# Layer 0's keys and values turned to rows by VectorE in 32x32 blocks instead of by TensorE

## The chip, the cores and the metric

The kernel runs on one core of a Trainium2 chip, in one launch. The metric is the time of the program on the device in microseconds (us); the core's engines (TensorE, VectorE, ScalarE, GpSimd, SyncE; PE, DVE, ACT, POOL and SP in the profile) run side by side, each through its own queue of instructions in order.

## What is computed

One step of a two-layer streaming encoder with 2,048 channels, for 512 new tokens of a prompt and 16 new tokens of each of 8 running streams (640 tokens in all). Layer 0 is stick-breaking attention, layer 1 gated linear attention. What matters here is the start of layer 0:

```python
h = rmsnorm(x, norm_g[i]) * (1 + scale[:, None]) + shift[:, None]
q, k, v, zg = jnp.split(h @ w_in, 4, axis=-1)          # each (tokens, 2048)
...
new_k.append(k)                                        # outputs: rows of tokens
new_v.append(v)
```

The keys `k` and the values `v` of all 640 tokens are outputs, token by token, as rows of 16 heads of 128 channels. The scale, shift and gate come from products of a conditioning vector with the matrix `w_ada`.

## The kernel before, in words

The projections of layer 0 are computed transposed: TensorE multiplies a block of the weight (as the stationary side) with the transposed activations, so that a result has channels on the 128 partitions and tokens along the free axis. `by_sevens` does this for 256 output channels at a time, with seven products in place of eight (a Strassen-like scheme over two halves of the tokens and two of the channels). One round of its loop is called a **job** here. A job has seven **products** of 24 matmuls (L592), each 320 tokens wide. Its result is `out`, two tiles of 128 channels by 640 tokens: `out[0]` is complete after the sixth product, `out[1]` after the seventh. There are 28 jobs in layer 0: for each of the eight pairs of heads the keys (K0 to K7) and the queries, from pair 2 on the values too (V2 to V7; those of pairs 0 and 1 are made elsewhere), and at the end six jobs of the gate. The order is K0 Q0 K1 Q1 K2 Q2 V2 K3 Q3 V3 and so on to V7.

A job's weights are four loads of 512 KB, issued by SP: three into tiles named `wb` (four buffers) and one into `wr`. Each waits until an earlier tile has been split into a high and a low part (ACT, L134, and DVE, L135), and a split waits until TensorE has freed a pair of split tiles. So the first `wb` of a round can go soon after the end of the job before, `wr` later, and the next `wb` only after the second product.

Beside the jobs two kinds of side work run, as lanes that a small planner (`Side`, with a clock of TensorE's work in the program) drops between half products. `rest_of_ada` multiplies `w_ada` with the conditioning vectors: 56 groups of eight short matmuls (L180 and L222), five half products apart, each of which uses two tiles `ar` of 512 KB. There are two `ar` buffers, so the loads for a group can start only when the group before is done. The lane has work up to job K7. The other lane is `as_rows`: after a key or value job it turns `out` to rows of tokens, in three steps one half product apart. A step has four (the last one two) transposes of 128x128 on TensorE into PSUM (L677); DVE copies the result to a tile `kr` (L858), and SP stores it (L74): `kr` to the output, and for values to the scratch tensor `vd` as well, which the attention reads later. A store moves rows of 256 channels, 1 KB at a time. The keys are also stored as they are, without a turn, to `kd` (`keep_in`).

The order of TensorE's instructions is the program's. Those of the other engines are put in order by a scheduler when the program is built. SP's queue is one queue: weight loads, `ar` loads and stores are issued in one order, and an instruction that waits holds up all behind it.

Of the kernel before, what the change touches and what calls it, by code (L numbers as in the profile page):

```python
# [8 lines left out]
F32 = mybir.dt.float32  # L9
# [6 lines left out]
P = 128  # L16
D = 2048
KT = D // P
NP = 512
# [22 lines left out]
def hybrid_step_kernel(ctx: ExitStack, tc: tile.TileContext, A: dict, O: list):  # L42
# [4 lines left out]
    dve = nc.vector  # L47
# [17 lines left out]
    def block(x):  # L65

        pe["now"] += 0.11
        return x
# [4 lines left out]
    def store(out, in_):  # L73
        nc.sync.dma_start(out=out, in_=in_)  # L74

    def move(out, in_):

        nc.gpsimd.dma_start(out=out, in_=in_)
# [20 lines left out]
    def bank(tag):  # L99
        return psum["pool"].tile([P, 512], F32, tag=tag, name=f"ps_{tag}", bufs=psum["bufs"][tag])  # L100
# [28 lines left out]
    v_d = [dp.tile([T, 256], F32, name=f"vd_{p}") for p in range(NPAIR)]  # L129
# [136 lines left out]
    def slot(n, shape=(P, T), dt=F32R, name="h"):  # L266
        return hp.tile(list(shape), dt, tag=f"t{n}", name=name)
# [6 lines left out]
    def step(wait=0.0, tp=0, z=0, tiled=False):  # L274
        return wait, tp, z, tiled

    class Side:
# [21 lines left out]
        def next(self, lane):  # L299
            what = next(lane[0], None)  # L300
            if what is None:
                self.lanes.remove(lane)
            else:
                lane[1] = (pe["now"] + what[0], {"tp": what[1], "z": what[2]}, what[3])
# [4 lines left out]
        def run(self, x):  # L309
            taken = {k: n for k, n in x[1][1].items() if n}  # L310
            self.next(x)
            for k, n in taken.items():
                f = sorted(self.free[k])
                self.free[k] = f[n:] + [pe["now"] + self.hold[k]] * n
# [29 lines left out]
    side = Side()  # L344

    def drive(*gens):
        for g in gens:
            for _ in g:
                side.tick()
# [311 lines left out]
    def keep_in(d):  # L661
        def f(out):
            for hh in range(2):
                store(d[:, hh, :], out[hh])
        return f

    def as_rows(out, leave):

        for g in range(3):
            yield step(3.0 if g == 0 else 0.5, tp=1)  # L670
            n = min(2, TOK - 2 * g)
            tp = bank("tp")
            for a in range(n):
                for hh in range(2):
                    c = 256 * a + P * hh
                    t0 = P * (2 * g + a)
                    turn_block(tp[:, c:c + P], block(out[hh][:, t0:t0 + P]), ident)  # L677
            leave(g, n, tp[:, :256 * n].rearrange("p (a n) -> p a n", n=256))
# [60 lines left out]
    kp_rows = kp_o.rearrange("l b t h d -> (l b t) (h d)")  # L739
    vp_rows = vp_o.rearrange("l b t h d -> (l b t) (h d)")  # L740
    ks_rows = ks_o.rearrange("l b t h d -> (l b t) (h d)")
    vs_rows = vs_o.rearrange("l b t h d -> (l b t) (h d)")
# [9 lines left out]
    with tc.tile_pool(name="st", bufs=1, reuse_waits="tile") as st:  # L752
# [21 lines left out]
        for a in range(TOK):  # L774
            ss4 = st.tile([P, 4], F32, tag="ss4", name="ss4", bufs=2)
            for q in range(4):
# [3 lines left out]
                tp = bank("mm")  # L780
# [8 lines left out]
            if a == 2:  # L789
                tp = bank("tp")  # L790
# [53 lines left out]
    def rest_of_ada():  # L844
        yield step(22.0)
        yield from ada_gate(ad, ad_ring, 0, "z", 2, cT)
        for k0 in range(0, 8, 2):
            yield from ada_mod(ad, ad_ring, 1, k0, 2, "z", 2)
        yield from ada_gate(ad, ad_ring, 1, "z", 2, cT, (0,))

    with tc.tile_pool(name="wq", bufs=1, reuse_waits="tile") as wq:
        def rows0(out, p, scratch, prompt, sample):

            cs = slice(256 * p, 256 * p + 256)

            def leave(g, n, tp):
                kr = slot(12 + g % 2, (P, 2, 256), F32, "kr")
                dve.tensor_copy(kr[:, :n, :], tp)  # L858
                if scratch is not None:
                    store(scratch[256 * g:256 * g + P * n, :].rearrange("(a p) n -> p a n", p=P), kr[:, :n, :])  # L860
                if g < 2:
                    store(prompt[256 * g:256 * g + 256, cs].rearrange("(a p) n -> p a n", p=P), kr)
                else:
                    store(sample[:, cs], kr[:, 0, :])

            return as_rows(out, leave)

        def keep_key(p):
            def f(out):
                keep_in(k_d[p])(out)  # L870
                side.add(rows0(out, p, None, kp_rows, ks_rows))
            return f

        def keep_value(p):
            return lambda out: side.add(rows0(out, p, v_d[p], vp_rows, vs_rows))

        jobs = []
        for p in range(NPAIR):
            jobs += [(D + 256 * p, keep_key(p)), (256 * p, keep_in(q_d[p]))]
            if p >= 2:  # L880
                jobs.append((2 * D + 256 * p, keep_value(p)))
        jobs += [(3 * D + 256 * p, keep_in(z_d[p])) for p in range(PLAIN, NPAIR)]
        side.every = 8.0
        side.add(rest_of_ada())
        ring3["pool"] = wq
        ring3["n"] = 0
        sevens = by_sevens(h1, w_in0, wq, jobs, given)
        for _ in range(2):
            next(sevens)
        for i in range(5):  # L890
            v01 = slot(8 + i, (P, 512), F32, "v01")
            (dve.tensor_copy if i % 2 else nc.scalar.copy)(v01, acc[i])
            for p in range(2):
                move(v_d[p][P * i:P * i + P, :], v01[:, 256 * p:256 * p + 256])
            move(vp_rows[P * i:P * i + P, 0:512] if i < 4 else vs_rows[:, 0:512], v01)
        ends.close()
        drive(sevens)
        side.finish()
        h1.again(0, wq)
        ring3["pool"] = None  # L900
# [326 lines left out]
    with tc.tile_pool(name="o0", bufs=1, reuse_waits="tile") as po, ExitStack() as only_d:  # L1227
# [3 lines left out]
        t = sp.tile([P, 1280], F32, tag="s2", name="c1")  # L1231
# [3 lines left out]
        t = sp.tile([P, 512], F32R, tag="s7", name="middles")  # L1235
# [184 lines left out]
        for nt in range(2):  # L1420
            x = low[nt][:32, :HALF]
# [28 lines left out]

        jobs = [(NK, keep_in(gk_d[0]))]
        jobs += [(2 * NK + 512 * h + 256 * n, keep_value(h, n)) for h in range(1, GH) for n in range(2)]
        jobs += [(2 * NK + D + 512 * h + 256 * n, keep_gate(h, n)) for h in range(GH) for n in range(2)]
        sevens = by_sevens(h2, w_in1, wq, jobs)
        next(sevens)
        n = 0
# [37 lines left out]
    with tc.tile_pool(name="gl", bufs=1, reuse_waits="tile") as gl:  # L1494
# [30 lines left out]
        t = mask_g[1].rearrange("p (b t) -> p b t", b=NB)  # L1525
# [61 lines left out]
        def leave(h, t0, on, g):  # L1587

            tp = bank("tp")
            for s in range(4):  # L1590
                turn_block(tp[:, P * s:P * s + P], block(on[:, P * s:P * s + P]), ident)
            dve.tensor_tensor(g, tp.rearrange("p (s t) -> p s t", s=4), g, op=ALU.mult)
            move(og_d[h][:, :, t0:t0 + P], g)
# [332 lines left out]
    with tc.tile_pool(name="o1", bufs=1, reuse_waits="tile") as po:  # L1926
# [3 lines left out]
        for kt in range(10, 16):  # L1930
            r = po.tile([P, T], F32, tag="rows", name="og_in", bufs=6)
            load(r, og_d[kt // 4][:, kt % 4, :])
            n = 20 + 2 * kt % 12
# [88 lines left out]
```

## Time and profile before

| | us |
|---|---|
| median of three runs (lowest, highest) | 2547.45 (2543.54, 2550.54) |
| the profiled execution: its time, and its span | 2556.43, 2554.7 |
| TensorE busy | 2442.0 (96%) |
| VectorE busy | 1582.3 (62%) |
| ScalarE busy | 995.3 (39%) |
| DMA queue of SP: share of the 16 DMA engines over the span | 54.4% |

The busy shares say that TensorE is what the kernel waits for nearly everywhere. Busy time of TensorE counts overlapping matmuls once; in the groups by line, a matmul's own duration overlaps with its neighbours', so what one costs is read from the distance of starts in the timeline. In a row of the timeline the columns are start, duration, engine, line, operation, tiles (written <- read), shape and count. The stage that the change touches, from K0's first transpose to V7's, lies between 187 and 794 us.

### The profile page before, as it was taken

Reading aid. Unit: us, or ns where it says so; the run is one execution under the profiler, and the core shown is the slowest. Engines: PE = TensorE matmul, PEld = TensorE weight load, DVE = VectorE, ACT = ScalarE, POOL = GpSimd, SP = SyncE. Lnnn points to the kernel's source line nnn. Section 1 sums busy time; section 2 is a strip of 40 time slices with the busy share of each in tenths; the row PEclk is TensorE's granted clock in tenths of the full one; section 3 lists DMA queues with packets and bytes.
Section 4 is the critical chain, followed back from the end, with each engine's and each line's share of the span. In section 5 each row is a group of like instructions: output and inputs, shape, how many; then the busy total and the mean of one; then the engine's idle time right before and its main releaser. Section 6 shows DMA issues by size and latency. Waiting matters only on the chain.

```text
span 2554.7 us, 43975 instructions
## 1 busy us (share of the span) xinstructions
PE 2442.0 (96%) x17561; PEld 2159.4 (85%) x17561; DVE 1582.3 (62%) x2565; ACT 995.3 (39%) x1730; POOL 164.1 (6%) x390
## 2 busy tenths in 40 slices
PE   6899999999999989999999989999999999979998
PEld 4589999998999989788887767999999988857776
DVE  5575555555666656666775677666766465555456
ACT  4332222222223334555442354333333464455223
POOL 0010000000000000000000000000000233243100
PEclk8899999999999999999999989999999999989999
DMA  9966666766654357778764753344444677785634
GB/s 341 321 211 210 223 212 201 239 215 196 220 186 122 118 188 236 248 245 253 255 211 123 232 184 114 105 121 139 118 115 117 209 230 244 228 283 191 210 117 147
DMA packets 469439, 503.13 MB, mean 197 GB/s; under 512 B 42730, under 2 KB 366450, under 8 KB 469106
## 3 DMA queue, kind: packets, MB, share of 16 engines
q1 hardware_dynamic: 446274, 436.60, 54.4%
q0 software_dynamic: 16048, 51.92, 6.1%
q10 hardware_dynamic: 6912, 11.80, 1.2%
q8 instruction: 138, 2.26, 0.4%
q14 instruction: 67, 0.55, 0.1%
HBM read 411.10 MB, written 89.13 MB: 196 GB/s over the span
## 4 chain that ended last, share of the span: by engine, by line
PE 77%; DMA 7%; DVE 5%; ACT 3%; issue 2%; POOL 0%; SPq 0%; ACTq 0%; POOLq 0%; DVEq 0%
PE ps_mm L592 39%; PE ps_mm L696 10%; PE ps_mm L650 7%; PE ps_mm L367 3%; PE ps_tp L1079 2%; PE ps_tp L1544 2%; DMA gv<-kr 1%; PE ps_mm L516 1%; PE ps_tp L1131 1%; PE ps_tp L1039 1%; PE ps_z L1015 1%; PE ps_z L180 1%; PE ps_mm L1993 1%; PE ps_z L1093 1%; PE ps_z L222 1%
## 5 line engine op out<-in xcount | busy, mean ns | idle before, releaser
L592 PE MATMUL ps_mm<-sums,wh 128*128 128x320 f32 x2752 | 616.5, 313 | 3.8 <-ACT wh L134 3.8
L592 PEld LDWEIGHTS ps_mm<-sums,wh 128*128 128x128 f32 x2752 | 460.8, 189 | 12.9 <-issue 7.4
L592 PE MATMUL ps_mm<-h,wh 128*128 128x320 f32 x2064 | 462.1, 312 | 2.1 <-DVE u L598 2.1
L592 PE MATMUL ps_mm<-sums,wl 128*128 128x320 f32 x1376 | 427.5, 311 | 1.1 <-DVE wl L135 1.1
L135 DVE TENSOR_TENSOR wl<-wr,wh 128x1024 fp32r<-128x1024 f32 x194 | 237.4, 1224 | 245.0 <-ACT wh L134 244.3
L592 PEld LDWEIGHTS ps_mm<-h,wh 128*128 128x128 f32 x2064 | 343.7, 188 | 17.7 <-issue 13.9
L134 ACT CAST wh<-wb 128x1024 fp32r<-128x1024 f32 x170 | 178.4, 1049 | 424.5 <-PE ps_mm L592 363.8
L134 ACT CAST wh<-wr 128x1024 fp32r<-128x1024 f32 x194 | 203.6, 1050 | 356.1 <-PE ps_mm L592 187.9
L592 PE MATMUL ps_mm<-h,wl 128*128 128x320 f32 x1032 | 319.3, 309 | 0.0
L650 PE MATMUL ps_mm<-h,wh 128*128 128x320 f32 x1152 | 268.8, 321 | 10.2 <-ACT wh L134 5.8
L592 PEld LDWEIGHTS ps_mm<-sums,wl 128*128 128x128 f32 x1376 | 259.8, 189 | 1.7 <-DVE wl L135 1.7
L135 DVE TENSOR_TENSOR wl<-wb,wh 128x1024 fp32r<-128x1024 f32 x170 | 207.9, 1223 | 59.6 <-ACT wh L134 59.3
L650 PEld LDWEIGHTS ps_mm<-h,wh 128*128 128x128 f32 x1152 | 195.6, 192 | 27.2 <-issue 12.3
L696 PE MATMUL ps_mm<-wh,ogh 128*128 128x512 f32 x460 | 201.5, 438 | 5.0 <-DVE y L701 4.0
L592 PEld LDWEIGHTS ps_mm<-h,wl 128*128 128x128 f32 x1032 | 194.0, 188 | 0.0
L696 PE MATMUL ps_mm<-wh,ogl 128*128 128x512 f32 x460 | 181.8, 395 | 0.3 <-DVE ogl L135 0.3
L696 PE MATMUL ps_mm<-wl,ogh 128*128 128x512 f32 x460 | 181.6, 395 | 0.0
L650 PE MATMUL ps_mm<-h,wl 128*128 128x320 f32 x576 | 180.2, 313 | 0.4 <-DVE wl L135 0.4
L696 PEld LDWEIGHTS ps_mm<-wh,ogh 128*128 128x128 f32 x460 | 87.2, 189 | 33.5 <-issue 18.7
L650 PEld LDWEIGHTS ps_mm<-h,wl 128*128 128x128 f32 x576 | 110.1, 191 | 0.8 <-DVE wl L135 0.8
L696 PEld LDWEIGHTS ps_mm<-wh,ogl 128*128 128x128 f32 x460 | 87.0, 189 | 20.6 <-DVE ogl L135 0.7
L516 PE MATMUL ps_mm<-wh,h 128*128 128x512 f32 x252 | 93.5, 433 | 4.3 <-ACT h L134 1.9
(355 smaller groups left out, 3736.0 us busy)
## 6 DMA issues: line engine op xcount, KB each, us to landing
ar<-in_w_ada_dram SPq DMA_DIRECT2D x160, 512.0 KB
wb<-in_sb_w_in_dram SPq DMA_DIRECT2D x82, 512.0 KB
kc<-in_cache_sb_k_dram SPq DMA_DIRECT2D x64, 512.0 KB
vc<-in_cache_sb_v_dram SPq DMA_DIRECT2D x64, 512.0 KB
wr<-in_gla_w_in_dram SPq DMA_DIRECT2D x51, 512.0 KB
wb<-in_gla_w_in_dram SPq DMA_DIRECT2D x45, 512.0 KB
wr<-in_sb_w_in_dram SPq DMA_DIRECT2D x44, 512.0 KB
ar<-in_w_ada_dram SPq DMA_DIRECT2D x64, 256.0 KB
```

The costliest lines, as they stand in the source:

```text
L134: nc.scalar.copy(hi, x)
L135: (e or dve).tensor_tensor(lo, x, hi.bitcast(F32), op=ALU.subtract)
L180: mm(acc[32 * q:32 * q + 32, :w], cT[:, kt + m, :], by(cT[:, kt + m, :], rs[m // each][:, m % each, q, :]), start=kt + m == 0, stop=kt + m ...
L222: mm(acc[32 * j:32 * j + 32, :256], cT[:, kt + m, :], by(cT[:, kt + m, :], r[:, 256 * j:256 * j + 256]), start=kt + m == 0, stop=kt + m == ...
L367: mm(acc[a], l[:, c], by(l[:, c], r[:, k2, :]), start=kt == k0 and first, stop=kt == k0 + nk - 1 and last)
L516: mm(acc[a], l, by(l, r[:, e, :]), start=j == 0 and e == 0 and begun, stop=j == 7 and e == 1 and last)
L592: mm(acc, l[:, k, :], by(l[:, k, :], r), start=start and k == 0 and first, stop=k == 7 and last, skip_group_check=True)
L650: mm(acc[nt], l[:, k, :], by(l[:, k, :], r), start=k0 == 8 and k == 0 and first, stop=k0 == 0 and k == 7 and last)
L696: mm(acc, l, by(l, r[:, e, :]), start=i == 0 and e == 0 and first, stop=i == 1 and e == 1 and last)
L1015: mm(z[:, :n], q[:, hh, qs], by(q[:, hh, qs], k[:, hh, :n]), start=True, stop=True)
L1079: turn_block(tp[:, P * c:P * c + P], block(kc[:, c, P * hh:P * hh + P]), ident)
L1544: mm(out, l[a], by(l[a], r[b]), start=start and n == 0, stop=stop and n == 2, skip_group_check=True)
```

## The change

The lane `as_rows` is no longer used in layer 0. Right at the end of a key or value job (or, for `out[0]`, when the scheduler finds it complete) DVE transposes `out[hh]`, 128x640, in blocks of 32x32 into a tile `kr` of the same shape: each block is turned in place, so that partition 32a+i then holds, for block b of 32 tokens, token 32b+i with channels 32a to 32a+31. Four partition groups a are stored apart, each as runs of 32 channels, that is 128 bytes:

```diff
-            cs = slice(256 * p, 256 * p + 256)
-
-            def leave(g, n, tp):
-                kr = slot(12 + g % 2, (P, 2, 256), F32, "kr")
-                dve.tensor_copy(kr[:, :n, :], tp)
-                if scratch is not None:
-                    store(scratch[256 * g:256 * g + P * n, :].rearrange("(a p) n -> p a n", p=P), kr[:, :n, :])
-                if g < 2:
-                    store(prompt[256 * g:256 * g + 256, cs].rearrange("(a p) n -> p a n", p=P), kr)
-                else:
-                    store(sample[:, cs], kr[:, 0, :])
-
-            return as_rows(out, leave)
+            def run(dst, x, c):
+                x = x.rearrange("i (b j) -> i b j", j=32)
+                store(dst.rearrange("(b i) n -> i b n", i=32)[:, :, c:c + 32], x)
+
+            for hh in range(2):
+                t = slot(12 + hh, dt=F32, name="kr")
+                dve.transpose(t, out[hh])
+                for a in range(4):
+                    x, c = t[32 * a:32 * a + 32, :], P * hh + 32 * a
+                    if scratch is not None:
+                        run(scratch, x, c)
+                    run(prompt, x[:, :NP], 256 * p + c)
+                    run(sample, x[:, NP:], 256 * p + c)
 
         def keep_key(p):
             def f(out):
                 keep_in(k_d[p])(out)
-                side.add(rows0(out, p, None, kp_rows, ks_rows))
+                rows0(out, p, None, kp_rows, ks_rows)
             return f
 
         def keep_value(p):
-            return lambda out: side.add(rows0(out, p, v_d[p], vp_rows, vs_rows))
+            return lambda out: rows0(out, p, v_d[p], vp_rows, vs_rows)
```

A key job then has 16 stores to the outputs in place of three (beside the two to `kd`, which stay), a value job 24 in place of six. The bytes are the same.

The order of the instructions shows what moves. First SP's queue after job V4. Before, from the first store of V4's rows on; `wb_5291` and `wr_5293` are weights of the next job but one, the tiles `ar` those of the next groups of the lane:

```order
L74 DMA vd_4_145<-kr_5325 128x2x256
L74 DMA out_3_dram<-kr_5325 128x2x256
L71 DMA wr_5293<-in_sb_w_in_dram 128x8x128
L71 DMA ar_5339<-in_w_ada_dram 128x2x512
L74 DMA vd_4_145<-kr_5363 128x2x256
L74 DMA out_3_dram<-kr_5363 128x2x256
L74 DMA vd_4_145<-kr_5383 128x256
L74 DMA out_5_dram<-kr_5383 128x256
L71 DMA wb_5291<-in_sb_w_in_dram 128x8x128
L71 DMA ar_5440<-in_w_ada_dram 128x2x512
L71 DMA ar_5442<-in_w_ada_dram 128x2x512
```

With the change, the last three of the 24 stores of V4's rows, which stand in one piece, and what follows them:

```order
L74 DMA vd_4_145<-kr_5275 32x20x32
L74 DMA out_3_dram<-kr_5275 32x16x32
L74 DMA out_5_dram<-kr_5275 32x4x32
L71 DMA wb_5301<-in_sb_w_in_dram 128x8x128
L71 DMA wb_5303<-in_sb_w_in_dram 128x8x128
L71 DMA wr_5305<-in_sb_w_in_dram 128x8x128
L71 DMA ar_5327<-in_w_ada_dram 128x2x512
L71 DMA ar_5329<-in_w_ada_dram 128x2x512
L71 DMA ar_5411<-in_w_ada_dram 128x2x512
L71 DMA ar_5413<-in_w_ada_dram 128x2x512
L71 DMA wb_5580<-in_sb_w_in_dram 128x8x128
```

Six stores between the loads have become 24 in a row, and the loads `ar_5327` and `ar_5329` stand behind all of them and behind three weight loads, two of them `wb`; before, loads of `ar` stood among the stores. After a key job the piece reads 16 stores with the two to `kd` among them, then `wb`, `wr` and two `ar`.

Second, TensorE after the same job. Before, from the end of the first product after V4 (`h_1605`) on:

```order
L592 MATMUL ps_mm_5281<-h_1605,wh_5203 128x320 x2
L592 MATMUL ps_mm_5281<-h_1605,wl_5204 128x320
L677 MATMUL ps_tp_5320<-ident_74,out_5017 128x128
L677 MATMUL ps_tp_5320<-ident_74,out_5018 128x128
L677 MATMUL ps_tp_5320<-ident_74,out_5017 128x128
L677 MATMUL ps_tp_5320<-ident_74,out_5018 128x128
L180 MATMUL ps_z_5047<-ar_5230,cT_151 32x256 x4
L180 MATMUL ps_z_5047<-ar_5232,cT_151 32x256 x4
L592 MATMUL ps_mm_5341<-sums_679,wh_5248 128x320 x2
```

With the change, from V4's last matmul (`sums_1637`) to the first group of the lane after it:

```order
L592 MATMUL ps_mm_5157<-sums_1637,wl_5159 128x320
L592 MATMUL ps_mm_5293<-h_613,wh_5199 128x320 x2
L592 MATMUL ps_mm_5293<-h_613,wl_5200 128x320
L592 MATMUL ps_mm_5293<-h_771,wh_5199 128x320 x2
L592 MATMUL ps_mm_5293<-h_771,wl_5200 128x320
L592 MATMUL ps_mm_5293<-h_962,wh_5199 128x320 x2
L592 MATMUL ps_mm_5293<-h_962,wl_5200 128x320
L592 MATMUL ps_mm_5293<-h_985,wh_5199 128x320 x2
L592 MATMUL ps_mm_5293<-h_985,wl_5200 128x320
L180 MATMUL ps_z_5102<-ar_5195,cT_151 32x256 x4
L180 MATMUL ps_z_5102<-ar_5197,cT_151 32x256 x4
```

The transposes are gone, and the group now stands 12 matmuls, half a product, behind the job's end. Sixty matmuls after it stands the next group, which reads the tiles `ar_5327` and `ar_5329` of SP's piece above:

```order
L592 MATMUL ps_mm_5293<-h_1607,wh_5294 128x320
L592 MATMUL ps_mm_5293<-h_1608,wh_5294 128x320
L592 MATMUL ps_mm_5293<-h_1607,wl_5295 128x320
L180 MATMUL ps_z_5102<-ar_5327,cT_151 32x256 x4
L180 MATMUL ps_z_5102<-ar_5329,cT_151 32x256 x4
L592 MATMUL ps_mm_5344<-sums_684,wh_5345 128x320 x2
```

## The prediction, on record before the run

> **What bounds the kernel now.** I read the page first, then the stage of the change by windows, then who waits there, then single instructions in the timeline. The page's head and its chain of work that ended last:
>
> ```profile
> span 2554.7 us, 43975 instructions
> PE 2442.0 (96%) x17561; PEld 2159.4 (85%) x17561; DVE 1582.3 (62%) x2565; ACT 995.3 (39%) x1730; POOL 164.1 (6%) x390
> ...
> PE ps_mm L592 39%; PE ps_mm L696 10%; PE ps_mm L650 7%; PE ps_mm L367 3%; PE ps_tp L1079 2%; PE ps_tp L1544 2%; DMA gv<-kr 1%; PE ps_mm L516 1%; PE ps_tp L1131 1%; PE ps_tp L1039 1%; PE ps_z L1015 1%; PE ps_z L180 1%; PE ps_mm L1993 1%; PE ps_z L1093 1%; PE ps_z L222 1%
> ```
>
> The stage from the first turned key to the last turned value, by windows, and TensorE's waits in it:
>
> ```profile
> core 0: us, PE busy (x) PEld busy (x) DVE busy (x) ACT busy (x) POOL busy (x), PEclk, DMA share, GB/s
> 187.00:790.00 603.00, 600.53 (x4553) 557.27 (x4552) 353.46 (x407) 168.29 (x190) 0.00 (x0) 1.00 0.65 206
> PE ps_tp L189 <- DVE ada_r L185: 2.1, 1, 2.1
> PE ps_z L222 <- DMA ar<-in_w_ada_dram: 0.4, 1, 0.4
> ```
>
> TensorE works 600.5 of 603 us. So whatever leaves its queue is gained in full, and whatever makes it wait is paid in full. It has no slack to hide anything. DVE is busy 59% (353/603) and the DMA engines 65%.
>
> **What goes: the transposes.** The group, and one of its places in the timeline:
>
> ```profile
> L677 PE MATMUL ps_tp<-ident,out x140: 270/273/273, 186.9 to 793.9; 128*128 128x128 f32 x140
> 387.74 0.46 PE L592 MATMUL ps_mm<-h,wh 128*128 128x320 f32 x2
> 388.03 0.31 PE L592 MATMUL ps_mm<-h,wl 128*128 128x320 f32 x1
> 388.18 0.60 PE L677 MATMUL ps_tp<-ident,out 128*128 128x128 f32 x4
> 388.53 0.54 PE L592 MATMUL ps_mm<-sums,wh 128*128 128x320 f32 x2
> ```
>
> The 273 ns of one transpose overlap with its neighbours. Starts tell the cost: matmuls follow at (388.03-387.74)/2 = 0.147 us, and from the last one before the four transposes to the next it is 0.50 us, so four cost 0.35 us, ten 0.88. 14 jobs: **-12.4 us**. This is certain, as TensorE does not wait there.
>
> **What comes on DVE.** No row shows the block transpose. The copies it replaces are 692 ns for 512 columns, and a 1,024-column subtraction takes 1,223 ns:
>
> ```profile
> L858 DVE COPY kr<-ps_tp 128x512 f32<-128x512 f32 x26 | 18.0, 692 | 22.8 <-PE ps_tp L677 19.4 <-DMA kd<-out 3.4
> L858 DVE COPY kr<-ps_tp 128x256 f32<-128x256 f32 x13 | 5.5, 422 | 11.5 <-DMA out_dram<-kr 11.2 <-PE ps_z L222 0.2
> L135 DVE TENSOR_TENSOR wl<-wb,wh 128x1024 fp32r<-128x1024 f32 x84 | 102.7, 1223 | 21.2 <-ACT wh L134 20.9
> ```
>
> 640 columns lie between 0.75 and 1.5 us (twice the rate's worth as the upper end); I take 0.8 us, as the copies' rate. Two make 1.6 us a job against 1.8 for the copies. DVE has 41% free and the splits run two products ahead, so even 1.5 us stay hidden: 0, and 0.7 us per job (10 us in all) if that lead were gone. I leave it at 0.
>
> **What comes on SP: the stores in one piece.** SP issues its DMAs in order, one in about 0.4 us:
>
> ```profile
> L74 SPq DMA_DIRECT2D out_dram<-kr x42: 356/424/2450, 188.2 to 796.4; - x42
> 447.27 0.37 SPq L74 DMA_DIRECT2D vd<-kr  x1
> 447.69 0.46 SPq L74 DMA_DIRECT2D out_dram<-kr  x1
> ```
>
> I take 0.45 us for each. 24 stores of a value job are 10.8 us, 18 of a key job 8.1. With time counted from the job's last matmul: `out[0]` is complete one product (24 x 0.147 = 3.5 us) earlier; 0.5 us for the last addition and 0.8 for the transpose, so the piece starts at -2.2 and ends at +8.6 (values) or +5.9 (keys).
>
> What do the packets cost? The stretch from 1252.1 to 1253.1 us has hardly anything but packets of 64 bytes, that from 421 to 424 us hardly anything but 512-byte rows of weights:
>
> ```profile
> DMA packets 1516, 0.10 MB, mean 96 GB/s; under 512 B 1516, under 2 KB 1516, under 8 KB 1516
> q1 hardware_dynamic: 1516, 0.10, 101.0%
> ...
> DMA packets 1040, 0.52 MB, mean 175 GB/s; under 512 B 16, under 2 KB 1040, under 8 KB 1040
> q1 hardware_dynamic: 1040, 0.52, 65.7%
> ```
>
> 1.01 x 16 engines x 1 us / 1,516 = 10.7 ns; 0.657 x 16 x 3 us / 1,040 = 30.3 ns. Both are loads; no row shows a store of so short rows. A run of 128 bytes lies between these two, by length near the first (13.6 ns); I take that. A value job stores 10,240 runs, 640 per engine: 8.7 us, under the 10.8 that SP needs to issue them. So the piece stays bound by SP. At 30.3 ns it would be 19.4 us.
>
> The Trainium skill ("DMA: Bandwidth & Descriptors", section Specifications) speaks against the change here: below 512 bytes a transfer becomes a read-modify-write and loses the line rate. No store in this trace is short enough to test it. By that rule the price is at least that of the 512-byte row, which is the last rival below.
>
> **Who waits behind the piece.** The `ar` loads. Before, after K4, in SP's and TensorE's timelines (L180 is the group that uses two `ar`):
>
> ```profile
> 473.06 0.91 SPq L71 DMA_DIRECT2D ar<-in_w_ada_dram  x2
> 474.25 0.37 SPq L71 DMA_DIRECT2D wb<-in_sb_w_in_dram  x1
> 476.58 0.38 SPq L74 DMA_DIRECT2D out_dram<-kr  x1
> 477.71 0.37 SPq L71 DMA_DIRECT2D wr<-in_sb_w_in_dram  x1
> 478.78 3.95 SPq L74 DMA_DIRECT2D out_dram<-kr  x2
> 483.51 0.38 SPq L71 DMA_DIRECT2D wb<-in_sb_w_in_dram  x1
> ...
> 472.36 1.07 PE L180 MATMUL ps_z<-ar,cT 128*32 128x256 f32 x16
> 475.23 0.60 PE L677 MATMUL ps_tp<-ident,out 128*128 128x128 f32 x4
> 481.69 1.07 PE L180 MATMUL ps_z<-ar,cT 128*32 128x256 f32 x16
> ```
>
> K4 ended at 475.23 - 3.52 - 1.05 = 470.7 (24 matmuls and the group lie between). The group freed its tiles at 473.06 and the next loads were issued at that moment, 8.6 us before their use. That is all the cover there is: a load needs about 2.5 us beyond its bytes (128 KB land 2.9 us after their issue on another queue, below) and a pair of `ar` 2 x 1.43 us (512 KB at 366 GB/s), 5.4 in all.
>
> ```profile
> vd<-v POOLq DMA_DIRECT2D x10, 128.0 KB, 2.9
> 945.00:949.00 4.00, 4.00 (x32) 4.00 (x32) 2.29 (x8) 3.02 (x7) 0.00 (x0) 1.00 1.08 366
> ```
>
> From the same rows: `wr` went at +7.0 and the second `wb` at +12.8, 3.8 us after the second product's end (+9.0 there). In the change after V4 that product ends at 2 x 3.52 + 1.05 = +8.1, so the second `wb` can go at +11.9 whatever the stores cost, and SP's order puts it and `wr` ahead of the `ar` pair. With 1.94 us for each weight load (64 packets per engine x 30.3 ns), the first `ar` lands at 11.9 + 2.5 + 1.94 + 1.94 + 1.43 = +19.7, the second at +21.1. The group stands half a product after V4, ends at +2.8, and the next stands 60 matmuls (8.8 us) on, at +11.6. TensorE waits 8.1 us for the first tile and 0.9 for the second: 9.0.
>
> The same working for the other jobs needs only the place of the group after the job's end, in the change's order of TensorE: 0 matmuls (end +1.0) for V2 and K6, 12 (+2.8) for K1, K3 and V4, 24 (+4.5) for K5 and V6, 36 (+6.3) for K2, K7 and V3, 48 (+8.1) for K0, K4 and V5; V7 has none. V6 (needed at +13.3): 6.4 + 0.9 = 7.3. V5 (needed at +16.9, second `wb` at +10.9 as no group delays the product): 1.8 + 0.9 = 2.7. V3, where one `ar` goes ahead of the second `wb`: 1.3, and 2.9 for the other, 4.2. V2, where one pair slips in after five stores: 0.9. After a key job only `wb` and `wr` (+7.0) stand before the pair, which lands at +13.7 and +15.1: K1 and K3 2.1 + 0.9 = 3.0 each, K5 1.3, the rest 0. **Sum +31.4 us.**
>
> **The clock.** The one long wait of this stage shows what follows a wait: after 2.1 us without work TensorE's granted clock is 0.51 for 3.4 us.
>
> ```profile
> 576.60:579.20 2.60, 0.52 (x5) 0.26 (x4) 2.46 (x3) 0.00 (x0) 0.00 (x0) 1.00 0.80 266
> 579.80:583.20 3.40, 3.40 (x15) 3.40 (x14) 0.93 (x6) 1.00 (x1) 0.00 (x0) 0.51 0.54 158
> ```
>
> Half of 3.4 us is 1.7 us lost again. Five of the waits above reach 2.1 us in one piece (V4, V6, V3, K1, K3): **+8.5 us**.
>
> The sum: -12.4 + 31.4 + 8.5 = +27.5 us. The profiled execution took 2556.43 us (span 2554.7 and 1.7 around it), 9 us above the median of 2547.45; it would take 2584, and the median **2575 us**.
>
> **The rivals.**
>
> Only what the second `wb` forces (chance 0.16). If SP and the rings deal with the stores faster than I think, K1, K3, K5, V2, V3 and V5 go without a wait, but V4 and V6 still have their pair behind a `wb` that comes at +11.9: 16.3 + 3.4 - 12.4 = +7.3, 2555 us. For it: TensorE waited only 0.4 us for an `ar` in the stage before. Against it: SP's pace is a row, and 18 of its issues do not fit into the cover left.
>
> All covered, the plain gain (chance 0.12): -12.4, 2535 us. This would be so if `ar` pairs still landed in time, that is within 8.6 us of the group before. For it speaks the DMA engines' free 35%. Against it: the order itself, in which the pair after V4 stands behind the second `wb`. It decides at V4.
>
> The short stores cost what a 512-byte row does, 30.3 ns or more (chance 0.22). Then DMA engines bound the piece: 19.4 us for values, to +17.2, and 9.7 for keys, to +8.0. The loads behind it land 7.3 us later after V4 (26.95 against 19.7), and the waits become V2 8.2, V3 12.8, V4 16.3, V5 11.0, V6 14.6, K1 and K3 5.1, K5 3.4, K2 and K7 1.6 each: 79.7, with eight half-clock stretches 13.6, less 12.4: +80.9, 2628 us. For it: no store so short was seen. Against: 64-byte loads ran at 10.7 ns.
>
> **The numbers.** The forecast has a chance of 0.50. The range runs from 2541 to 2628: below it lies most of the plain gain, above it short stores that cost more than 30 ns, together under 2 in 10. About 0.3% (7.6 us) is what a measurement of this kernel tells from no change. Faster comes from the plain gain alone, 0.12; within 0.3% from the second rival, 0.16; slower from the forecast and the short stores, 0.72.
>
> **What would show it.** Right: no L677 before 800 us; SP's stores of `kr` 0.4 to 0.5 us apart; PE or PEld waits for DMA `ar` of 5 to 9 us after V4 and V6, of 2 to 4 after K1, K3 and V3, and the clock at half after them; packets of 128 bytes near 14 ns. Wrong: no waits for `ar` (then -12 us is left), or stores spaced by over 0.7 us (then the DMA engines bound them), or DVE waiting for `kr` to be stored, for which I reckon nothing, since it is 28 us old by then.

## The result and the profile after

The changed kernel takes **2597.99 us** (median of 6 runs, 2586.47 to 2601.11) against 2552.8 us for the kernel before in the runs beside it (2543.54 to 2560.8): a ratio of **1.017, 95% interval 1.0152 to 1.0189**, so 45 us slower by the medians. The profiled executions differ by less, 2592.08 us against 2556.43. The forecast was 2575, that is +27.5 us on the 2547.45 of the first three runs: the sign and the mechanism came out, and all three terms of the sum were too small in size.

The page of the changed kernel, its busy times and the costliest links of the chain that ended last:

```profile
PE 2442.5 (94%) x17421; PEld 2153.8 (83%) x17421; DVE 1582.2 (61%) x2551; ACT 995.9 (38%) x1730; POOL 163.2 (6%) x390
...
PE ps_mm L592 37%; PE ps_mm L696 9%; PE ps_mm L650 7%; PE ps_mm L367 3%; DMA ar<-in_w_ada_dram 3%; PE ps_tp L1079 2%; PE ps_tp L1544 2%; PE ps_tp L1131 1%; PE ps_mm L516 1%; PE ps_tp L1039 1%; PE ps_z L1015 1%; SPq L74 1%; PE ps_z L180 1%; PE ps_z L1093 1%; PE ps_mm L1993 1%
```

TensorE does 140 instructions less (17,421 for 17,561) and is busy just as long as before (2442.5 for 2442.0 us). `DMA ar` and `SPq L74`, SP's issue of the stores, are new among these links. To see where the time went I take the stage from the first to the last matmul of layer 0's rounds (L592), a window for each kernel. Of before:

```profile
154.83:934.67 779.84, 775.22 (x5748) 730.63 (x5747) 466.18 (x527) 226.65 (x259) 7.70 (x18) 1.00 0.61 192
```

Of after:

```profile
151.70:975.55 823.85, 778.88 (x5608) 726.42 (x5607) 465.90 (x513) 226.79 (x259) 7.71 (x18) 0.97 0.62 182
```

Columns: length, then busy time of PE, PEld, DVE, ACT and POOL, granted clock, share of the DMA engines. The stage is **44.0 us longer** (823.85 - 779.84), as much as the medians differ. TensorE idles 45.0 us in it (823.85 - 778.88) where it idled 4.6: +40.4. It is busy 3.7 us longer although 140 transposes are gone, and the granted clock fell from 1.00 to 0.97. DVE, ACT and POOL do the same as before. The remaining 8 us by which the two profiles differ less than the stages lie outside it, where nothing was changed.

TensorE's waits for `ar` from 187 to 840 us in the changed kernel (us in total, times, the longest):

```profile
PE ps_z L180 <- DMA ar<-in_w_ada_dram: 26.5, 12, 8.6
PE ps_z L222 <- DMA ar<-in_w_ada_dram: 14.8, 8, 7.3
```

Before, the `ar` loads cost 0.4 us there. Now they cost 41.3 us, and hardly anything else there makes TensorE wait (1.5 us). SP's timeline behind V4, whose last product ends at 542.0, shows what the loads stood behind:

```profile
539.93 0.33 SPq L74 DMA_DIRECT2D vd<-kr  x1
540.32 1.06 SPq L74 DMA_DIRECT2D out_dram<-kr  x2
...
548.55 2.22 SPq L74 DMA_DIRECT2D out_dram<-kr  x2
...
552.88 1.08 SPq L74 DMA_DIRECT2D out_dram<-kr  x2
554.07 1.02 SPq L71 DMA_DIRECT2D wb<-in_sb_w_in_dram  x2
555.14 1.20 SPq L71 DMA_DIRECT2D wr<-in_sb_w_in_dram  x1
556.44 2.09 SPq L71 DMA_DIRECT2D ar<-in_w_ada_dram  x2
```

24 stores take SP from 539.93 to 553.96, then come three weight loads, then the pair of `ar`, 14.4 us after the end of V4. TensorE's timeline at the two groups that need this pair:

```profile
562.35 1.08 PE L180 MATMUL ps_z<-ar,cT 128*32 128x256 f32 x8 [8.58 <-DMA ar<-in_w_ada_dram]
563.61 1.08 PE L180 MATMUL ps_z<-ar,cT 128*32 128x256 f32 x8 [0.18 <-DMA ar<-in_w_ada_dram]
```

### The profile page after: what moved, and what is told of

Its sections match the earlier page's. It is cut to its first block, busy times and chain, and to the rows that moved or that the text cites. A ratio compares the mean times of both kernels' runs of the same rounds, so it can differ in the third digit from the quotient of the medians.

```text
span 2590.4 us, 43936 instructions
## 1 busy us (share of the span) xinstructions
PE 2442.5 (94%) x17421; PEld 2153.8 (83%) x17421; DVE 1582.2 (61%) x2551; ACT 995.9 (38%) x1730; POOL 163.2 (6%) x390
## 4 chain that ended last, share of the span: by engine, by line
PE 73%; DMA 8%; DVE 5%; issue 3%; ACT 2%; SPq 2%; POOL 1%; ACTq 0%; POOLq 0%; DVEq 0%
PE ps_mm L592 37%; PE ps_mm L696 9%; PE ps_mm L650 7%; PE ps_mm L367 3%; DMA ar<-in_w_ada_dram 3%; PE ps_tp L1079 2%; PE ps_tp L1544 2%; PE ps_tp L1131 1%; PE ps_mm L516 1%; PE ps_tp L1039 1%; PE ps_z L1015 1%; SPq L74 1%; PE ps_z L180 1%; PE ps_z L1093 1%; PE ps_mm L1993 1%
## 5 line engine op out<-in xcount | busy, mean ns | idle before, releaser
L592 PE MATMUL ps_mm<-sums,wh 128*128 128x320 f32 x2752 | 622.8, 315 | 3.8 <-ACT wh L134 3.8
L592 PEld LDWEIGHTS ps_mm<-sums,wh 128*128 128x128 f32 x2752 | 467.3, 191 | 20.2 <-issue 16.0
L592 PE MATMUL ps_mm<-h,wh 128*128 128x320 f32 x2064 | 461.4, 312 | 2.3 <-DVE u L598 1.2
L592 PE MATMUL ps_mm<-sums,wl 128*128 128x320 f32 x1376 | 430.3, 313 | 1.2 <-DVE wl L135 1.2
L592 PEld LDWEIGHTS ps_mm<-h,wh 128*128 128x128 f32 x2064 | 345.4, 189 | 13.3 <-issue 9.4
L592 PE MATMUL ps_mm<-h,wl 128*128 128x320 f32 x1032 | 319.6, 310 | 0.0
L650 PE MATMUL ps_mm<-h,wh 128*128 128x320 f32 x1152 | 270.3, 322 | 10.6 <-ACT pl L1504 3.8
L592 PEld LDWEIGHTS ps_mm<-sums,wl 128*128 128x128 f32 x1376 | 262.9, 191 | 1.9 <-DVE wl L135 1.9
L592 PEld LDWEIGHTS ps_mm<-h,wl 128*128 128x128 f32 x1032 | 194.5, 188 | 0.0
L598 DVE TENSOR_TENSOR u<-ps_mm,m 128x320 f32<-128x320 f32 x86 | 42.1, 489 | 94.6 <-PE ps_mm L592 94.6
```

Source lines behind the costliest of these rows:

```text
L592: mm(acc, l[:, k, :], by(l[:, k, :], r), start=start and k == 0 and first, stop=k == 7 and last, skip_group_check=True)
L598: dve.tensor_tensor(o, pt, x, op=ALU.add)
L650: mm(acc[nt], l[:, k, :], by(l[:, k, :], r), start=k0 == 8 and k == 0 and first, stop=k0 == 0 and k == 7 and last)
```

## The experiments

**Theory A**, the prediction's: the loss is made in SP's in-order queue, by the number of stores that stand in one piece ahead of the `ar` loads. **Rival B**: the short packets load the DMA engines. **Rival C**: VectorE's transposes, or other waits in the place of these. In the diffs `store` issues from SP, `move` from POOL, `nc.scalar.dma_start` from ACT. Stage, PE busy and PE idle are from windows as above, in us, from the first to the last matmul of the rounds.

| kernel | ratio to before, 95% interval | stage | PE busy | PE idle |
|---|---|---|---|---|
| before | 1 | 779.8 | 775.2 | 4.6 |
| changed | 1.017 (1.0152 to 1.0189) | 823.9 | 778.9 | 45.0 |
| e1_pool_queue | 1.031 (1.029 to 1.033) | 857.8 | 769.6 | 88.2 |
| e2_few_packets | 1.0137 (1.0106 to 1.0168) | 814.5 | 778.3 | 36.2 |
| e3_few_issues | 0.9962 (0.995 to 0.9974) | 767.0 | 760.6 | 6.4 |
| e4_transposes_doubled | 1.0108 (1.0082 to 1.0134) | 797.1 | 789.9 | 7.2 |
| e4b_doubled_layer0 | 1.0062 (1.0038 to 1.0086) | 798.9 | 792.8 | 6.1 |
| e5_spread | 0.9983 (0.9969 to 0.9997) | 778.4 | 764.5 | 13.9 |
| e5b_spread_faster | 0.9995 (0.9982 to 1.0008) | 778.8 | 764.1 | 14.7 |
| e6_ar_apart | 0.9997 (0.9977 to 1.0018) | 783.7 | 766.7 | 17.0 |
| e8_spread_ar_apart | 1.0024 (1.0005 to 1.0043) | 788.8 | 767.5 | 21.3 |
| f2_spread_sample_on_act | 0.9944 (0.9929 to 0.996) | 765.4 | 759.5 | 5.9 |

**e2_few_packets: as many issues, fewer packets.**

```diff
-                    run(prompt, x[:, :NP], 256 * p + c)
-                    run(sample, x[:, NP:], 256 * p + c)
+                    run(prompt[:32], x[:, :32], 256 * p + c)
+                    run(sample[:32], x[:, NP:NP + 32], 256 * p + c)
```

> The changed kernel, in which each prompt and each sample store carries only its first block of 32 tokens (32 packets, not 512 or 128): the rest of those outputs is left out. Scratch stores are whole. SP issues as many DMAs as in the changed kernel, a value job moves 5,632 packets of 128 bytes, not 10,240, a key job 512, not 5,120. Theory A (issues): stores stay 0.45 us or more apart, ar waits stay at 30 us or more, 2580 to 2598. Rival B (packets): ar waits under 15 us, 2540 to 2560.

Measured: 2586.75 us. TensorE's waits for `ar` from 187 to 840 us:

```profile
PE ps_z L180 <- DMA ar<-in_w_ada_dram: 22.1, 13, 7.3
PE ps_z L222 <- DMA ar<-in_w_ada_dram: 9.7, 4, 6.3
```

With half to a tenth of the packets 31.8 of 41.3 us of `ar` waits remain, and 34 of the 45 us. So the packets left out are worth about a quarter of the loss, and three quarters stay with as many issues, as A expects. The quarter fits a faster SP: with fewer packets two `out_dram` stores take it 0.97 us instead of 1.07, and V4's piece ends 10.6 us after the job instead of 12.0.

**e3_few_issues: as many packets, fewer issues.** The reverse test (`apart_d` holds scratch buffers of 128x20x64 in DRAM, one for each head; the lines for prompt and sample leave the loop over `a`, the new ones stand behind it):

```diff
-                    run(prompt, x[:, :NP], 256 * p + c)
-                    run(sample, x[:, NP:], 256 * p + c)
+                x = t.rearrange("i (b j) -> i b j", j=32)
+                apart = apart_d.pop()
+                store(apart[:, :16, :32], x[:, :16])
+                store(apart[:, 16:, :32], x[:, 16:])
```

> The changed kernel, in which prompt and sample stores of a head go as one DMA of 128 partitions each, in the same packets of 128 bytes, to a scratch buffer: those outputs are left out. The packets are as many and as long as in the changed kernel, SP's issues fall from 24 to 12 after a value job and from 18 to 6 after a key job. Theory A: a piece ends about 6 us sooner, so the waits after K1, K3, K5, V3 and V5 go, those after V4 and V6 are set by the second wb (7 us together with it): 2545 to 2562. Rival B: as the changed kernel, 2590 to 2605.

Measured: 2542.58 us, 10 us **faster** than before, and the `ar` waits are nearly gone. TensorE's only waits of that stretch, then SP's timeline behind V4 (its last product ends at 519.6):

```profile
PE ps_z L181 <- DMA ar<-in_w_ada_dram: 4.2, 4, 1.8
```

```profile
523.57 1.50 SPq L74 DMA_DIRECT2D apart<-kr  x2
525.17 0.47 SPq L71 DMA_DIRECT2D wb<-in_sb_w_in_dram  x1
525.75 1.08 SPq L71 DMA_DIRECT2D ar<-in_w_ada_dram  x2
...
530.08 0.37 SPq L71 DMA_DIRECT2D wb<-in_sb_w_in_dram  x1
```

As many packets of 128 bytes, in half the issues, leave SP free 5.5 us after V4's end instead of 12 (+5.5 for +12 in what follows), and the pair goes at +6.2. The time lies below A's 2545 to 2562, and the reason is in the last rows: the pair now stands *ahead* of the second `wb`, which I had reckoned would hold it. B, as a cause by itself, falls with this run: all the packets, none of the loss. So does C for VectorE's transposes, which are all here.

**e1_pool_queue: the same stores from another queue.**

```diff
-                store(dst.rearrange("(b i) n -> i b n", i=32)[:, :, c:c + 32], x)
+                move(dst.rearrange("(b i) n -> i b n", i=32)[:, :, c:c + 32], x)
```

> The changed kernel, with all stores of kr issued from POOL's DMA queue and not from SP's: the same transposes, the same packets of 128 bytes, the same DMA count, but nothing of it ahead of the ar loads in SP's order. Theory A (the loss is SP's in-order issue of the 24 or 18 stores, behind which the ar loads stand): the waits for ar fall from 41 us to under 10, the time to between 2540 (the plain gain of 12.4 us against 2552) and 2560 (if the second wb still holds the pairs after V4 and V6, +7). Rival B (the short packets load the DMA engines): still near 2598, ar waits near 41 us. Rival C (VectorE's transposes or the order of TensorE): still near 2598, with other waits in the place of ar.

Measured: 2629.81 us, slower than the change itself. TensorE's longest waits, and those for `ar`:

```profile
PE ps_mm L592 <- DVE wl L135: 69.3, 4, 18.7
PE ps_mm L592 <- DVE u L598: 13.9, 2, 13.3
PE ps_z L222 <- DMA ar<-in_w_ada_dram: 1.9, 1, 1.9
```

The `ar` waits are gone as A says, 1.9 for 41.3 us. Something else took their place, which I had put under rival C for other reasons. POOL's timeline, and the group of VectorE's transposes from 330 to 960 us (busy, mean ns, idle before them and its releaser):

```profile
365.77 1.20 POOL L78 DMA_DIRECT2D out_dram<-kr  x2 [5.15 <-issue]
368.23 0.70 POOL L78 DMA_DIRECT2D vd<-kr  x1 [1.27 <-issue]
374.23 1.21 POOL L78 DMA_DIRECT2D out_dram<-kr  x2 [5.29 <-issue]
377.41 0.69 POOL L78 DMA_DIRECT2D vd<-kr  x1 [1.97 <-issue]
```

```profile
L860 DVE STREAM_TRANSPOSE kr<-out 128x640 f32<-128x640 f32 x22 | 18.6, 845 | 121.8 <-DMA out_dram<-kr 121.4
```

POOL issues a store in 0.6 to 0.7 us, but after every one or two lets 1.3 to 5.3 us go by for nothing that the profile names. Six stores took from 365.77 to 378.10, 2 us each, and 24 at that pace need about 50 us, where the next job with stores ends some 25 us later. So the two `kr` tiles are still being stored when VectorE wants to write them again. It waits 121 us for that in its own order, with `wl` and `u` queued behind, for which TensorE then waits 83 us.

**e5_spread, e5b_spread_faster: the same issues on SP, not in one piece.** `rows0` becomes a generator in the side lane, as the code before had it, and pauses behind each group of two or three stores (2.5 us, in e5b 1.2; values in the same way):

```diff
                     run(sample, x[:, NP:], 256 * p + c)
+                    yield step(2.5)
...
-                rows0(out, p, None, kp_rows, ks_rows)
+                side.add(rows0(out, p, None, kp_rows, ks_rows))
```

> The changed kernel, whole, with the stores of a job not in one piece: after each of the eight groups (one head, one block of 32 dimensions: two or three stores) the code goes back to the side lane for 2.5 us, so that the loads of ar and of weights come between them in SP's order. SP issues as many DMAs, and the packets are the same. Theory A (it is the piece ahead of ar in SP's order that costs): at most 1.5 us of stores stand ahead of a pair, the ar waits fall from 41 to under 12 us, 2540 to 2560. Rival B (SP as a whole, or the DMA engines, have no room for so many stores): 2580 to 2605. Rival C (stores that end later hold kr, and VectorE's next transposes wait as they did on POOL's queue, with wl behind them): over 2600, with PE waits for wl.

> As e5_spread, with 1.2 us in the place of 2.5 between the groups of stores: the stores of a job then stand nearer together, but still in groups of two or three. Theory A: between the piece and e5_spread, ar waits 5 to 25 us, 2548 to 2575. If only the room for one pair of loads between stores counts, as e5_spread, 2545 to 2552.

Measured: 2548.99 us with 2.5 us, 2550.59 with 1.2 (ratio 0.9995, interval 0.9982 to 1.0008), so either spacing serves, and SP has room for all 24 stores. The waits in e5_spread:

```profile
PE ps_mm L592 <- DVE u L598: 4.2, 4, 1.6
PE ps_z L180 <- DMA ar<-in_w_ada_dram: 4.0, 7, 1.9
...
PE ps_z L222 <- DMA ar<-in_w_ada_dram: 0.7, 1, 0.7
```

`ar` costs 4.7 us for 41.3 with not a store or a packet less: it is their place in the queue that costs, not their number as such.

**e6_ar_apart, e8_spread_ar_apart: only the `ar` loads leave SP.** The piece stays as it is:

```diff
+    def fetch(out, in_):
+        nc.scalar.dma_start(out=out, in_=in_)
...
-                    load(r, src[:, k, 2 * D + 1024 * hf:2 * D + 1024 * hf + 1024])
+                    fetch(r, src[:, k, 2 * D + 1024 * hf:2 * D + 1024 * hf + 1024])
```

(and the loads of layer 1's modulation in the same way; e8 adds e5's pauses).

> The changed kernel, whole, with only the ar loads of the side work (gate columns and layer 1's modulation) issued from ACT's queue and not from SP's; the stores stay in one piece on SP. Theory A: the ar waits fall from 41 us to under 10, as nothing of kr stands ahead of them; ACT is 28% busy in the stage and pays about 0.4 us per load: 2538 to 2560. Rival B (the loads are late because of the DMA engines or because rings serve the stores first): ar waits of 25 us or more stay, 2580 or more. Rival C (ACT waits in its order for TensorE or VectorE before it gets to the load): ar waits of 10 to 30 us, 2555 to 2590.

> Both edits at once: stores spread over the job as in e5_spread, ar loads on ACT's queue as in e6_ar_apart; whole. Theory A: each of the two alone takes the ar waits away, so both together bring hardly more than the better one: 2538 to 2555, the plain gain of 12.4 us at best. If the two add up, each alone left part of the loss: then it lies under both by 5 us or more.

Measured: 2554.9 and 2561.93 us (ratio of e8 1.0024, interval 1.0005 to 1.0043). In e6 the `ar` waits vanish from TensorE's list, and a smaller wait appears. TensorE's largest wait in total, then VectorE's timeline at the longest of its times (brackets: idle before, releaser) and TensorE's:

```profile
PE ps_mm L595 <- DVE u L601: 11.7, 5, 4.4
...
```

```profile
396.55 1.23 DVE L558 TENSOR_TENSOR t<-wb 128x1024 f32<-128x1024 f32 x1 [7.33 <-DMA wb<-in_sb_w_in_dram]
...
398.95 0.48 DVE L601 TENSOR_TENSOR u<-ps_mm,m 128x320 f32<-128x320 f32 x1
...
399.58 0.87 PE L595 MATMUL ps_mm<-h,wh 128*128 128x320 f32 x2 [4.36 <-DVE u L601]
```

The weights' loads still stand behind the piece. VectorE comes to `t`, for which `wb` hasn't landed, and waits 7.33 us; the addition `u` stands behind `t` in its order, and TensorE waits 4.36 us for `u`. So a piece in SP's queue has a second victim, once the first one is out of the way. That e8 isn't the best of both goes against my expectation: TensorE waits 9.9 us for `u` and 6.7 for `out` there. In both kernels the `ar` pairs go out beside the weights and not behind them, and share the DMA engines with them. That this delays `wb` fits the trace, but isn't shown to be the cause.

**f2_spread_sample_on_act: the version that beats both.** e5_spread, with the eight sample stores of a job on ACT's queue (`run` takes the function that stores as an argument):

```diff
-                    run(sample, x[:, NP:], 256 * p + c)
+                    run(sample, x[:, NP:], 256 * p + c, nc.scalar.dma_start)
```

> As e5_spread, with the eight sample stores of a job issued from ACT's queue: SP issues 16 stores after a value job, 8 after a key job, ACT eight more of some 0.4 us each (about 3 of 25.7 us in a job, 28% of it busy before). Theory A: the ar waits left in e5_spread (4.7 us) and the waits for u behind late weights (4.2 us) shrink, 2538 to 2548. Rival: ACT's casts come late behind its DMAs, TensorE waits for wh or wl, 2550 or more.

Measured: **2538.65 us**, 15 us under the kernel before (ratio 0.9944, interval 0.9929 to 0.996). All waits of TensorE in the stretch, and the stage:

```profile
PE ps_mm L592 <- DVE u L598: 1.3, 2, 0.7
PE ps_tp L189 <- DVE ada_r L185: 1.2, 1, 1.2
PE ps_z L180 <- DMA ar<-in_w_ada_dram: 1.0, 1, 1.0
...
151.80:917.20 765.40, 759.54 (x5609) 713.72 (x5607) 464.05 (x513) 226.82 (x259) 7.76 (x19) 1.00 0.67 196
```

ACT's own issues are short:

```profile
L856 ACTq DMA_DIRECT2D out_dram<-kr x112: 322/382/1007, 177.2 to 773.6; - x112
```

This is the change's gain without its price: TensorE idles 5.9 us in the stage, about as before, and is busy 15.7 us less.

**e4_transposes_doubled, e4b_doubled_layer0: the price of the transposes by themselves,** on the kernel before (`times` is 2, in e4b for layer 0 only).

```diff
-                    turn_block(tp[:, c:c + P], block(out[hh][:, t0:t0 + P]), ident)
+                    for _ in range(times):
+                        turn_block(tp[:, c:c + P], block(out[hh][:, t0:t0 + P]), ident)
```

> The kernel before, with each of its 140 transposes of layer 0's keys and values made twice (the second writes the same block again). By the prediction's first step each costs 0.088 us of a TensorE that has no slack: +12.4 us against the kernel before, 2565, and no new waits. Rival: what a transpose takes is hidden or its row's 273 ns counts in full: 0, or +38 us.

> The kernel before, with the 140 transposes of layer 0's keys and values alone made twice; the 60 of layer 1 that e4_transposes_doubled doubled as well are single again. If a transpose costs what e4_transposes_doubled gives for each of its 200 (24.5 us by the medians, 20.5 by the profiles: 0.10 to 0.12 us), this costs 14 to 17 us: 2567 to 2570. By the prediction's 0.088 us it is 12.4, 2565. If the cost lay in layer 1's 60, this is within 3 us of the kernel before.

Measured: 2577.24 and 2570.82 us, +24.5 and +17.1. The first doubled 200 transposes, not 140: `as_rows` also serves layer 1, which I had overlooked when I wrote its expectation. That is why e4b was run. In both, the stage of layer 0 holds just 140 more, and it is 17.3 and 19.1 us longer, TensorE busy 14.6 and 17.6 us longer. Rival values of 0 and 38 us are out. The medians alone don't exclude the prediction's 12.4 (e4b's interval is 9.7 to 22 us), but e4b's timeline does. Four transposes took 0.35 us from the first of them to the next product's start, and eight take 0.79:

```profile
451.18 1.04 PE L678 MATMUL ps_tp<-ident,out 128*128 128x128 f32 x8
451.97 0.54 PE L592 MATMUL ps_mm<-sums,wh 128*128 128x320 f32 x2
```

Each further one costs 0.11 us, not 0.088, which is 15.4 us for 140.

## Why the prediction came true, and where its sizes failed

What the 44.0 us of the stage consist of follows from three windows. f2 does the same work on TensorE as the changed kernel, with hardly a wait, so the difference of their busy times is what the slower clock took: 778.88 - 759.54 = 19.3. Before against f2 is 775.22 - 759.54 = 15.7. Of these 1.5 us aren't the transposes' but the clock's: before has one stretch at half clock too (3.40 us of work at 579.80, shown in the prediction; 45% of it is lost, as worked out below), and f2 has none, as its longest matmul of L592 takes 0.42 us, where a single one at half clock takes 0.47. That leaves 14.2 us for the transposes, and 19.3 - 1.5 = 17.8 for what the change adds at half clock.

| term | forecast | measured |
|---|---|---|
| transposes gone | -12.4 | -14.2 |
| waits for `ar` (idle of TensorE) | +31.4 | +40.4 |
| clock after the waits | +8.5 | +17.8 |
| sum | +27.5 | +44.0 |

**TensorE has no slack.** Right: f2 gains what leaves the queue in full, the changed kernel pays all that it waits.

**Transposes: -12.4, called certain.** Too small by about 2 us. I took the time from the last matmul ahead of a group to the first one behind it, and left out that this first pair itself is slow. In before's timeline:

```profile
388.53 0.54 PE L592 MATMUL ps_mm<-sums,wh 128*128 128x320 f32 x2
388.91 0.31 PE L592 MATMUL ps_mm<-sums,wl 128*128 128x320 f32 x1
389.05 0.46 PE L592 MATMUL ps_mm<-sums,wh 128*128 128x320 f32 x2
389.35 0.31 PE L592 MATMUL ps_mm<-sums,wl 128*128 128x320 f32 x1
```

The pair behind the transposes takes 0.38 us to the next start, the following one 0.30. That is 0.08 us for each of 42 groups, 3.4 us. With these the working gives 15.8, near e4b's 15.4 and a little over the 14.2 of the windows.

**VectorE's transposes: 0.8 us, hidden.** Right: 845 ns, and in the changed kernel no TensorE wait for them. e1 shows the cover's limit: `kr` must have been stored before it is written again.

**SP: 0.45 us a store.** Too small. Two `out_dram` stores take 1.07 us, and the pieces of values have stalls like the 2.22 us at 548.55, for which no row names a cause. V4's 24 stores took 14.0 us, 0.58 each. The piece ended at +12.0, not +8.6. The pieces of K1, K3, K5 and K7 ended at +6.8 to +8.4, not +5.9. The waits that came out longer than forecast are those behind such pieces.

**A packet of 128 bytes: 13.6 ns; the piece is bound by SP.** Right, and the price was even high. From 541 to 547 us the changed kernel moves nothing but these stores:

```profile
DMA packets 5080, 0.63 MB, mean 104 GB/s; under 512 B 5080, under 2 KB 5080, under 8 KB 5080
q1 hardware_dynamic: 5080, 0.63, 60.9%
```

0.609 x 16 x 6 us / 5,080 = 11.5 ns, and the DMA engines are free for 39% of a stretch in which SP does nothing but issue. The Trainium skill ("DMA: Bandwidth & Descriptors", section Specifications) says that a transfer below 512 bytes becomes a read-modify-write and loses the line rate. On the rate the trace agrees: 128 bytes in 11.5 ns are 11 bytes per ns, against 512 in 30.3, 17 per ns. That a short store costs more than a long one, as the rival built on it had it, no run bears out.

**The waits for `ar`: 31.4 us.** The list was right at its head: V4 9.0 forecast, 8.6 + 0.2 measured; V6 7.3, and 7.3 + 0.2. V5 was 2.7 and became 3.9, V3 4.2 and 6.1, K1 3.0 and 4.2, V2 0.9 and 2.6, K7 0 and 2.2, K2 0 and 1.0; K3 and K5 grew by 0.3 and 0.5. These grew because their piece ended later than reckoned. That V4 and V6 came out to the size is luck, because the reason given for them isn't borne out: that the second `wb` can only go at +11.9 and holds the pair. In before and in e3 this load goes at the very end of VectorE's split `wl<-wb` (483.51 behind 483.48, 530.08 behind 530.06). In the changed kernel after V4 that split ends at 552.45, which is +10.5 (after V6 at 744.12, +10.4):

```profile
551.22 1.23 DVE L135 TENSOR_TENSOR wl<-wb,wh 128x1024 fp32r<-128x1024 f32 x1 [0.37 <-ACT wh L134]
```

SP came to the load at 554.57 only, when the piece had ended at +12.0. So the piece held the pair, and not the split. The +12.8 after K4 from which I had worked out +11.9 held a wait of the old code's own: just ahead of the split VectorE had a copy to `kr` to make, and waited 1.54 us for a store of `kr`:

```profile
481.92 0.42 DVE L858 COPY kr<-ps_tp 128x256 f32<-128x256 f32 x1 [1.54 <-DMA out_dram<-kr]
482.26 1.22 DVE L135 TENSOR_TENSOR wl<-wb,wh 128x1024 fp32r<-128x1024 f32 x1
```

A `wb` reckoned too late and a piece reckoned too short came to the same 12 us. In e3 the piece ends at +5.5, the pair goes at +6.2 and the second `wb` behind it at +10.5: nothing but SP's order makes the pair stand behind that load. The order of SP's queue is made anew for each kernel, and with a shorter piece it puts the pair first.

**The clock: five places of 1.7 us, +8.5.** The largest error in proportion. The granted clock was at half in nine stretches. Three of them by windows:

```profile
378.50:381.91 3.41, 3.41 (x14) 3.41 (x14) 1.89 (x2) 0.00 (x0) 0.00 (x0) 0.50 0.80 255
467.20:477.44 10.24, 7.39 (x36) 5.70 (x37) 2.45 (x2) 0.00 (x0) 0.00 (x0) 0.50 0.80 265
556.00:566.24 10.24, 3.71 (x22) 2.02 (x23) 2.46 (x3) 0.00 (x0) 0.00 (x0) 0.50 0.89 290
```

The stretch at 378.5 follows V2's two waits:

```profile
376.46 0.64 PE L180 MATMUL ps_z<-ar,cT 128*32 128x256 f32 x8 [1.93 <-DMA ar<-in_w_ada_dram]
377.73 0.64 PE L180 MATMUL ps_z<-ar,cT 128*32 128x256 f32 x8 [0.64 <-DMA ar<-in_w_ada_dram]
```

Each is under the 2.1 us from which I had counted, and so K5 and K7 have one too. K2's waits of 0.39 and 0.59 us brought none. And the stretches aren't all 3.4 us long: those of V3's and V4's waits last 10.24 us, three times as much, of which TensorE worked 7.39 and 3.71. In all nine it worked 40.3 us at half the clock. What a matmul loses there the timeline shows:

```profile
254.14 0.73 PE L592 MATMUL ps_mm<-sums,wh 128*128 128x320 f32 x2
...
254.94 0.73 PE L592 MATMUL ps_mm<-sums,wh 128*128 128x320 f32 x2
```

Three products in 0.80 us (254.14 to 254.94) instead of 0.44 make 45%, or 18 us of the 40.3, near the 19.3 by difference.

**The rivals.** "All covered", 2535 us, is wrong for this order of SP's queue and nearly right for another one, with the stores spread and the sample's on ACT's queue: f2 gives 2538.65. "Only what the second `wb` forces" fell with e3. "Short stores cost 30.3 ns" fell with the packets, at 11.5 (its keys' piece, too, would end at -2.2 + 9.7 = +7.5 and not +8.0, which is 2.5 us less in its sum). The measured time, 2598, lies between its 2628 and the forecast's 2575, but not for its reason: the pieces end late because SP issues more slowly, with DMA engines that are 39% free.

## What to carry to other kernels

Count the DMA *issues* that an edit adds to a queue, not only its bytes: a store that a 32x32 transpose cuts into four costs four places in an in-order queue, and what pays is the next load behind them. Freed engine time is kept only if what comes instead is spread between the loads, or shared out among queues with room, and a queue is to be tested for its own pace first (SP 0.58 us a store, POOL 2 us). On an engine without slack a wait costs more than its length: here 40 us of waiting cost another 18 us at half clock.

## What the runs showed of the hardware

- POOL's queue took 0.6 to 0.7 us to issue one of these stores and paused 1.3 to 5.3 us between them, where SP went on at 0.58 us, stalls included. Why POOL pauses no run tells.
- ACT's queue issued a store of 128 short packets in 0.38 us (median of 112 in f2), and TensorE had no wait for ACT's casts in the stretch.
- A VectorE transpose of 128x640 fp32 in 32x32 blocks takes 845 ns, every time (845 to 847).
- The first pair of matmuls behind a group of transposes on TensorE takes some 0.08 us more than those after it (0.38 us to the next start for 0.30), and each further transpose in a group costs 0.11 us.
- Two waits of 1.93 and 0.64 us, 0.6 us of work apart, were enough for 3.41 us of half clock; two of 0.39 and 0.59 us brought none.
